# A two-layer encoder on one core: the products of U of layer 0 dealt out between those of the last four gate groups, the latents sent through DRAM, the w_ada tiles placed anew

## The chip, the core and the metric

The kernel runs on one core of a Trainium2 chip. The core has a matrix engine (TensorE, PE in the profile, with its weight loads as PEld), VectorE (DVE), ScalarE (ACT), GpSimd (POOL) and SyncE (SP), which here issues most DMAs. The metric is the device time of one execution in microseconds (us), the median over several runs. All results of TensorE go to PSUM, eight banks of 128 partitions by 512 words, from which VectorE and ScalarE take them.

## The reference

```python
for l in range(DEPTH):                       # DEPTH = 2, 512 positions, D = 2048
    mod = c_act @ w_ada[l] + b_ada[l]        # w_ada[l]: 2048 x 6144
    shift, scale, gate = jnp.split(mod, 3, axis=-1)
    h = _layernorm(x) * (1.0 + scale[:, None, :]) + shift[:, None, :]
    p = h @ w_in[l]
    u_f, z_f, cq, ckv, k_r, z_a = jnp.split(p, split_pts, axis=-1)  # 1024, 1024, 512, 256, 64, 1024
    y_f = _fourier_mix(u_f, w_fmix[l]) * jax.nn.silu(z_f)
    q = (_rmsnorm(cq, q_norm[l]) @ w_q_b[l]).reshape(B, S, N_HEADS, QK_HEAD_DIM)
    ...
    k_rope = _apply_rope(k_r, cos, sin)
    y_a = _mla_attention(q_nope, q_rope, k_nope, k_rope, v) * jax.nn.silu(z_a)
    y = jnp.concatenate([y_f, y_a], axis=-1) @ w_out[l]
    x = _layernorm(DEEPNORM_ALPHA * x + gate[:, None, :] * y, ln_g[l], ln_b[l])
```

All values are float32. `_fourier_mix` is a Fourier transform over the 512 positions and over the 128 channels of each of eight groups, real part, then a linear map for each group.

## The kernel before

Every float32 product is made of three products (`mm3`, L151 to L153) of a high and a low half; `split` makes the halves, the high one as a cast on ScalarE (L147) and the low one as a subtraction on VectorE (L148). So each weight tile is loaded by SP into `wr`, cast, subtracted, and then used.

**Layer 0, w_in.** The modulation of layer 0 comes out of w_ada, which is read while w_in is already worked on. So w_in is taken in five steps of 1, 2, 3, 4 and 6 blocks of 128 rows (`SZ`). Each step goes through six groups of columns: CQ (512 columns), CKV (320), and four gate groups of 512, ZF (two, for the Fourier half) and ZA (two, for attention). The sums of a group are added up in SBUF from step to step (L1063), except CQ, whose four banks are kept. In the last step the order is CQ, CKV, ZA0, ZA1, ZF0, ZF1 (`LAST`), each of three units of two row blocks; a gate unit is 24 products 512 wide, so a group 72.

**w_ada.** A tile of w_ada (512 KB) is scaled by c and added to a sum by VectorE (L247). `k_group` asks for tiles by credits (`bg_step`): in steps 0 to 3 those that the next step needs at an even pace, then `ZP` for each unit; in the last step `ZL` for each unit; `AP` in attention, `CP` in the output projection. When a block of tiles is complete, `finish` runs two or three calls of `bg_step` later: transposes on TensorE (L260), a reduction (L261) and an addition (`modT`, L221) on VectorE. The next step starts with `make_h`, which is ScalarE's scaling by `modT` (L364) and a split.

**U.** U is h times the 1024 columns of u_f, with the channels of each group folded into sums and differences (`fold_unit`, 16 units of one row block, each two operations of VectorE at L401 and L402, a split 1024 wide, and `xacc`, L412); h is folded over positions too (`first_eo`, L613 to L615, and a split 512 wide). In before, all 16 units stand in one place (`u_pass`) behind the last gate group and the small products of `folded_constants` (L539): for each of two halves of positions three products go into one bank of the pool `pa` with 264 columns, three into another with 504, and three into a bank of `pm` with 256, so 18 products a unit. `pa` and `pm` have four banks each. Then come the evacuation of U, `fourier_folded` (its first products are those of `pa` 256 wide and `pm` 258 wide), the rotary queries, and attention.

**Latents.** `latent_q` and `latent_kv` evacuate and normalise the results of CQ and CKV; their second parts transpose them (`to_feat`) as work between the units of the next group (`runner`). `rotary_key` (L853 to L858) stands in between.

**Order.** All units of weights stand in one `Stream`; taking one also loads and converts those that stand some places ahead (`st.ahead(raw, conv)`: two converted ahead at first, `UA0` before and in U). The conversions of the units to come are so written ahead of the products of the unit taken, and of what evacuates their banks. The build makes one fixed order for each engine out of that; each engine works through its own and waits for the others by semaphores.

## Time and profile before

| what | value |
|---|---|
| time before, three runs | median 1418.49 us (1417.31 to 1423.09) |
| profiled execution | 1409.84 us, span 1408.0 us |
| PE busy in the span | 1317.0 us (94%) |
| DVE, ACT, POOL busy | 1040.7 us (74%), 601.2 us (43%), 59.6 us (4%) |
| chain that ended last | PE 38%, issue 4%, DVE 2%, DMA 2%, ACT 1% |

The span runs from the first to the last instruction of the profiled execution; 1.84 us of its time lie outside. A product's busy time is longer than its distance to the next one, since they overlap, so short waits of PE don't show in its busy share; where products follow each other, the distance of their starts is the measure. In lists by time a number in brackets is what the engine stood idle before that row, and what ended it.

### The profile page before, as it was taken

What the parts mean: (1) busy time and instruction counts of PE and PEld (TensorE: products, weight loads), DVE (VectorE), ACT (ScalarE), POOL (GpSimd) and SP (SyncE); (2) the same over time, 40 slices, a digit from 0 to 9 for tenths busy, and PEclk for the clock granted to TensorE, in tenths of its full rate; (3) what the DMA queues carried; (4) which work ended last, traced back from release to release, by engine and by line L of the source; (5) the groups of instructions that cost most, each with busy time, mean ns of one, the idle gap of its engine ahead of it and who ended that gap; (6) DMA issues with size and microseconds to landing.
All of it is one profiled execution on the core that took longest, in us unless ns stands there. A gap on an engine that the chain in (4) does not pass through costs nothing. (4 is left out here: it accounts for less than half of the span.)

```text
span 1408.0 us, 18682 instructions
## 1 busy us (share of the span) xinstructions
PE 1317.0 (94%) x6837; PEld 1114.3 (79%) x6837; DVE 1040.7 (74%) x1748; ACT 601.2 (43%) x1131; POOL 59.6 (4%) x87
## 2 busy tenths in 40 slices
PE   4889999998698999999997999999999999999996
PEld 3767788877587888787876888887898888888885
DVE  7999994779987898689878758557755577632448
ACT  6621333655526776211147525323234677721210
POOL 1000000010000000000021001011100000000001
PEclk9999999999999999999998999999999999999998
DMA  8989872565665245988736435359544221263313
GB/s 272 327 272 309 298 248 85 165 200 180 193 224 164 69 162 194 326 307 318 275 115 224 157 102 164 106 199 354 175 124 118 78 67 53 75 240 103 92 60 120
DMA packets 134772, 257.45 MB, mean 183 GB/s; under 512 B 19532, under 2 KB 50392, under 8 KB 134680
## 3 DMA queue, kind: packets, MB, share of 16 engines
q1 hardware_dynamic: 127640, 232.92, 50.3%
q0 software_dynamic: 7040, 23.34, 4.8%
q8 instruction: 54, 0.88, 0.2%
q14 instruction: 38, 0.31, 0.1%
HBM read 239.42 MB, written 16.79 MB: 182 GB/s over the span
## 5 line engine op out<-in xcount | busy, mean ns | idle before, releaser
L151 PE MATMUL pa<-b,b 128*128 128x512 f32 (+3 forms) x1472 | 549.4, 376 | 30.2 <-ACT b L147 16.3
L152 PE MATMUL pa<-b,b 128*128 128x512 f32 (+3 forms) x1472 | 549.3, 373 | 7.2 <-DVE ln_v L188 4.3
L153 PE MATMUL pa<-b,b 128*128 128x512 f32 (+3 forms) x1472 | 546.7, 372 | 0.5 <-DVE b L148 0.5
L151 PEld LDWEIGHTS pa<-b,b 128*128 128x128 f32 x1472 | 278.6, 191 | 83.5 <-ACT b L147 23.7
L152 PEld LDWEIGHTS pa<-b,b 128*128 128x128 f32 x1472 | 279.9, 190 | 54.1 <-DVE b L148 5.9
L153 PEld LDWEIGHTS pa<-b,b 128*128 128x128 f32 x1472 | 279.4, 190 | 47.6 <-DVE b L148 1.9
L147 ACT CAST b<-wr 128x1024 fp32r<-128x1024 f32 (+3 forms) x166 | 162.6, 991 | 325.8 <-PE pa L153 173.8
L148 DVE TENSOR_TENSOR b<-wr,b 128x1024 fp32r<-128x1024 f32 (+3 forms) x166 | 188.7, 1144 | 132.9 <-PE pa L152 68.6
L247 DVE SCALAR_TENSOR_TENSOR acc<-ada,cact,acc 128x1024 f32<-128x1024 f32 (+2 forms) x193 | 226.6, 1181 | 14.6 <-DMA ada<-in_w_ada_dram 12.6
L151 PE MATMUL pm<-b,b 128*128 128x256 f32 (+3 forms) x500 | 167.5, 335 | 7.2 <-DVE b L1063 5.7
L152 PE MATMUL pm<-b,b 128*128 128x256 f32 (+3 forms) x500 | 161.9, 324 | 0.0
L153 PE MATMUL pm<-b,b 128*128 128x256 f32 (+3 forms) x500 | 161.6, 323 | 0.0
L151 PEld LDWEIGHTS pm<-b,b 128*128 128x128 f32 x500 | 96.4, 193 | 19.5 <-issue 4.8
L153 PEld LDWEIGHTS pm<-b,b 128*128 128x128 f32 x500 | 96.4, 193 | 6.8
L152 PEld LDWEIGHTS pm<-b,b 128*128 128x128 f32 x500 | 96.5, 193 | 6.5
L148 DVE TENSOR_TENSOR b<-pm,b 128x512 fp32r<-128x512 f32 (+4 forms) x104 | 60.7, 606 | 22.7 <-ACT b L147 22.3
L147 ACT CAST b<-pm 128x512 fp32r<-128x512 f32 (+4 forms) x104 | 51.8, 529 | 50.5 <-PE pm L751 28.6
L147 ACT CAST b<-b 128x1024 fp32r<-128x1024 f32 (+1 forms) x48 | 43.2, 912 | 60.2 <-DVE b L402 50.0
L148 DVE TENSOR_TENSOR b<-b,b 128x1024 fp32r<-128x1024 f32 (+1 forms) x48 | 49.5, 1042 | 13.8 <-ACT b L147 13.8
L147 ACT CAST b<-t 128x512 fp32r<-128x512 f32 (+1 forms) x81 | 40.9, 531 | 26.3 <-DVE t L1021 13.7
L148 DVE TENSOR_TENSOR b<-t,b 128x512 fp32r<-128x512 f32 (+1 forms) x81 | 45.0, 576 | 8.2 <-ACT b L147 7.9
L987 ACT ACTIVATE t<-pa,mx 128x512 f32<-128x512 f32 x64 | 44.1, 695 | 4.8 <-DVE mx L984 4.7
(180 smaller groups left out, 1251.7 us busy)
## 6 DMA issues: line engine op xcount, KB each, us to landing
wr<-in_w_in_dram SPq DMA_DIRECT2D x107, 512.0 KB, 3.9
ada<-in_w_ada_dram SPq DMA_DIRECT2D x96, 512.0 KB, 5.8
wr<-in_w_out_dram SPq DMA_DIRECT2D x64, 512.0 KB, 4.4
ada<-in_w_ada_dram SPq DMA_DIRECT2D x96, 256.0 KB, 4.7
ada<-in_w_ada_dram POOLq DMA_DIRECT2D x32, 512.0 KB, 5.4
b<-in_x_dram SPq DMA_DIRECT2D x16, 512.0 KB, 6.7
t<-szd SPq DMA_DIRECT2D x32, 256.0 KB, 4.2
ada<-in_w_ada_dram SPq DMA_DIRECT2D x32, 192.0 KB, 4.4
```

The lines of the kernel that those rows point to most:

```text
L147: A.copy(hi, src)
L148: V.tensor_tensor(lo, src, f(hi), op=ALU.subtract)
L151: PE.matmul(o, lh, rh, start=first, stop=False)
L152: PE.matmul(o, lh, rl, start=False, stop=False)
L153: PE.matmul(o, ll, rh, start=False, stop=last)
L247: V.scalar_tensor_tensor(out=a, in0=t[:, r - r0], scalar=cact[:, r:r + 1], in1=a, op0=ALU.mult, op1=ALU.add)
L987: A.activation(e, ps, AF.Exp, bias=mx, accum_out=ssum)
```

## The change

The 16 units of U go between the twelve units of the last four gate groups: after gate unit m, `UPAT[m]` units of U (0, 1, 1, 2, 1, 1, 2, 2, 1, 2, 1, 2). Their sums stay open all that time, in all four banks of `pm`; each bank holds 260 columns of the even half and 252 of the odd half, so a unit is 24 products 260 or 252 wide. The transposes of the latents would need `pm`, so `latent_q` and `latent_kv` write the normalised latents to DRAM and read them back ahead of the last gate group, where the rotary key and the loads for `folded_constants` stand now too. Behind U come its evacuation, `folded_constants` and the transposes. In layer 1, U takes the same four banks and 24 products a unit. The numbers for w_ada change: `ZP` from 0.3 to 0, `ZL` from 0.5 to 1.6 but only in CQ and CKV of the last step, with none in its four gate groups, `AP` from 1.2 to 1.4, `CP` from 2.3 to 2.4. Two memsets go from VectorE to GpSimd.

```diff
-    ZP, ZL, AP, CP, G0, G1 = 0.3, 0.5, 1.2, 2.3, 0.8, 1.6
+    ZP, ZL, AP, CP, G0, G1 = 0.0, 1.6, 1.4, 2.4, 0.8, 1.6
...
-    FW, UAH, UA0, YS = 2, 6, 4, 4
+    FW, UAH, UA0, YS = 2, 6, 3, 4
+
+    UPAT = [0, 1, 1, 2, 1, 1, 2, 2, 1, 2, 1, 2]
...
         def conv(t):
             if act is not None:
-                h[k] = act(k)
+                he[k] = act(k)
             w, hi, lo = big([P, 1024], F32), big([P, 1024]), big([P, 1024])
             c = t.rearrange("p (g c) -> p g c", c=P)
             e = w[:, 0:512].rearrange("p (g c) -> p g c", c=64)
...
     for l in range(DEPTH):
         if l == 0:
             for k0, nk in STEPS:
-                for g in FIRST if k0 + nk < NK else LAST:
+                last, m, ku = k0 + nk == NK, 0, 0
+                for g in LAST if last else FIRST:
                     for k, n in pairs(k0, nk):
                         st.add(dense(w_in[l], k * P, *g, n))
-            for k in range(NK):
-                st.add(fold_unit(w_in[l], k, lambda k: first_eo(k)))
+                        if last and g in ZA + ZF:
+                            for _ in range(UPAT[m]):
+                                st.add(fold_unit(w_in[l], ku, lambda k: first_eo(k)))
+                                ku += 1
+                            m += 1
             for k in range(2):
                 st.add(wq_unit(l, 4 * k, 4, 128, 64))
         else:
...
         yf = []
-        def u_pass():
-
-            e, o, b = [pa(), pa()], [pa(), pa()], [pm(), pm()]
-            for k in range(NK):
-                wh, wl = st.next()
-                for p in range(2):
-                    es, os_ = slice(p * P, p * P + P), slice(256 + p * P, 256 + p * P + P)
-                    for bank, ts, cs in ((e[p], es, slice(256, 520)), (b[p], es, slice(0, 256)),
-                                         (o[p], os_, slice(520, 1024))):
-                        mm3(bank[:, :cs.stop - cs.start], h[k][:, 0, ts], h[k][:, 1, ts], wh[:, cs], wl[:, cs],
-                            k == 0, k == NK - 1)
+        def u_start():
+            return [[pm(), pm()] for _ in range(2)]
+
+        def u_step(banks, k):
+
+
+            wh, wl = st.next()
+            hk = (h if l else he)[k]
+            for p in range(2):
+                for x in range(2):
+                    ts = slice(256 * x + p * P, 256 * x + p * P + P)
+                    n = 252 if x else 260
+                    for b in range(2):
+                        cs = slice(520 * x + b * n, 520 * x + b * n + n)
+                        mm3(banks[p][b][:, 260 * x:260 * x + n], hk[:, 0, ts], hk[:, 1, ts], wh[:, cs], wl[:, cs],
+                            k == 0 and x == 0, k == NK - 1 and x == 1)
+
+        def u_finish(banks):
             un = big([P, 2, 2, 2, P])
             GP.memset(f(un), 0.0)
             ue, uo = [], []
             for p in range(2):
+                a, b = banks[p]
                 t = big([P, 2, 512])
-                split(t[:, 0, 256:512], t[:, 1, 256:512], e[p][:, 0:256])
-                split(un[:, 0, p, 0, 120:128], un[:, 0, p, 1, 120:128], e[p][:, 256:264])
+                split(t[:, 0, 0:260], t[:, 1, 0:260], a[:, 0:260])
+                split(t[:, 0, 260:512], t[:, 1, 260:512], b[:, 0:252])
+                split(un[:, 0, p, 0, 120:128], un[:, 0, p, 1, 120:128], b[:, 252:260])
                 ue.append(t)
-            for p in range(2):
                 t = big([P, 2, 8, 64])
-                split(t[:, 0, :, 1:64], t[:, 1, :, 1:64], o[p][:, :504].rearrange("p (g c) -> p g c", c=63))
-                for a in range(2):
-                    V.memset(f(t[:, a, :, 0]), 0.0)
+                for i, ps in enumerate((a, b)):
+                    gs = slice(4 * i, 4 * i + 4)
+                    split(t[:, 0, gs, 1:64], t[:, 1, gs, 1:64], ps[:, 260:512].rearrange("p (g c) -> p g c", c=63))
+                for x in range(2):
+                    GP.memset(f(t[:, x, :, 0]), 0.0)
                 uo.append(t.rearrange("p a g c -> p a (g c)"))
-            for p in range(2):
-                split(ue[p][:, 0, 0:256], ue[p][:, 1, 0:256], b[p][:, 0:256])
             onesr = t2([P, P], F32R)
             V.memset(f(onesr), 1.0)
...
         cq, ckv, krs = [], [], []
+        def stash(p, i, n):
+            for tb in range(NT):
+                SP.dma_start(lat[i * NT + tb, :, :n], p[tb][:, :n])
+
+        def unstash(i, n):
+            t = [big([P, 2, n], F32) for _ in range(2)]
+            p = [t[tb // 2][:, tb % 2] for tb in range(NT)]
+            for tb in range(NT):
+                SP.dma_start(p[tb], lat[i * NT + tb, :, :n])
+            return p
+
         def latent_q(src):
             p = latent(src, 512, 512)
+            if l == 0:
+                stash(p, 0, 512)
+                yield
+                p = unstash(0, 512)
             yield
             cq.extend(to_feat(p, k) for k in range(4))
         def latent_kv(src):
             p = latent(src, 256, 320)
+            if l == 0:
+                stash(p, 1, 320)
+                yield
+                p = unstash(1, 320)
             kb = rotary_key(p)
             yield
             ckv.extend(to_feat(p, k) for k in range(2))
...
                         w = st.next()
                         p_ = min(pace, left[0])
                         left[0] -= p_
-                        bg_step(p_ if p_ > 0 else 0 if g == LAST[-1] and final else ZL if final else ZP)
+                        bg_step(p_ if p_ > 0 else ZP if not final else ZL if g in (CQ, CKV) else 0)
                         if g in ZF or g in ZA:
                             fm_half(banks, w, h, k, k == k00, k + nr == k01)
                         else:
...
                 lq = latent_q(k_group(CQ, keep))
                 next(lq)
-                lkv = latent_kv(k_group(CKV, pas(), runner(lq)))
+                lkv = latent_kv(k_group(CKV, pas()))
                 next(lkv)
+                finish_late()
+                st.ahead(4, UA0)
+                ub, ku, todo_u = None, 0, iter(UPAT)
+
+                def u_steps():
+                    nonlocal ub, ku
+                    for _ in range(next(todo_u)):
+                        if ub is None:
+                            ub = u_start()
+                        u_step(ub, ku)
+                        ku += 1
+
                 for i, (g, dst) in enumerate(zip(LAST[2:], (0, 1, 2, 3))):
                     if i == 3:
-                        finish_late()
-                        st.ahead(4, UA0)
-                    zs = k_group(g, pas(), runner(lkv) if i == 0 else lambda: None)
+                        next(lq)
+                        next(lkv)
+                        raw = constants_raw(0)
+                    zs = k_group(g, pas(), u_steps)
                     for j in range(4):
                         A.activation(zs[j], zs[j], AF.Silu)
                     spill(dst, zs)
+                st.ahead(4, 2)
+                u = u_finish(ub)
+                cw, nq, dt = folded_constants(0, raw)
+                drain(lq)
                 drain(lkv)
-                cw, nq, dt = folded_constants(0)
-                u = u_pass()
-                st.ahead(4, 2)
                 fb, rq = fourier_folded(u), rotary_queries(1)
                 for i in range(8):
                     next(fb, None)
...
             unfolded(banks, H)
             cw, nq, dt = folded_constants(1)
             st.ahead(4, 2)
-            fb = fourier_folded(u_pass())
+            ub = u_start()
+            for k in range(NK):
+                u_step(ub, k)
+            fb = fourier_folded(u_finish(ub))
             unfolded(fm_group(runner(fb, FW)), H + 4)
             drain(fb)
             gt = gates()
```

Lines of the changed kernel stand some lines lower: L148 is L150 there, L247 is L250, L260 and L261 are L263 and L264, L364 is L367, L412 is L415, L539 is L550, L1063 is L1101.

The first place is TensorE where the third of the five steps ends (ZA1, `pm`) and the fourth begins. These rows of before are the end of ZA0 of the third step, with the transposes of the modulation behind it and ZA1 still to come (`acc` is the sum of w_ada tiles):

```order
L151 MATMUL pm_1205<-b_923,b_1172 128x512
L152 MATMUL pm_1205<-b_923,b_1172 128x512
L153 MATMUL pm_1205<-b_923,b_1173 128x512
L260 MATMUL pm_1274<-ident,acc_866 128x128 x4
L260 MATMUL pm_1280<-ident,acc_866 128x128 x4
L151 MATMUL pm_1263<-b_913,b_1206 128x512
L152 MATMUL pm_1263<-b_913,b_1206 128x512
```

And these are the end of ZA1 of the third step in the changed kernel, with CQ of the fourth step (`pa`, the halves of h in b_1331) behind it:

```order
L153 MATMUL pm_1261<-b_919,b_1237 128x512
L263 MATMUL pm_1300<-ident,acc_928 128x128 x4
L154 MATMUL pm_1261<-b_919,b_1237 128x512
L155 MATMUL pm_1261<-b_919,b_1238 128x512
L153 MATMUL pm_1262<-b_919,b_1237 128x512
L154 MATMUL pm_1262<-b_919,b_1237 128x512
L155 MATMUL pm_1262<-b_919,b_1238 128x512
L263 MATMUL pm_1306<-ident,acc_928 128x128 x4
L153 MATMUL pa_366<-b_1263,b_1331 128x512
L154 MATMUL pa_366<-b_1264,b_1331 128x512
```

The transposes went from ahead of ZA1 to its end, directly ahead of the products that need h of the fourth step.

On VectorE, the rows that follow those transposes in the changed kernel are the reductions (L264), the last two additions to ZA1's sums, `modT`, two tiles of w_ada, and the low halves of h:

```order
L264 TENSOR_REDUCE red_1299<-pm_1306 128x4
L1101 TENSOR_TENSOR b_595<-b_595,pm_1262 128x512
L224 TENSOR_TENSOR modT_133<-red_1299,vecT 128x2x4
L250 SCALAR_TENSOR_TENSOR acc_1355<-ada_1460,cact,acc_1355 128x1024
L250 SCALAR_TENSOR_TENSOR acc_1355<-ada_1464,cact,acc_1355 128x1024
L150 TENSOR_TENSOR b_1331<-t_1329,b_1331 128x512
L150 TENSOR_TENSOR b_1336<-t_1334,b_1336 128x512
```

In before the same rows have one tile of w_ada ahead of `modT` and two behind it, and ZA1's own additions stand behind the halves of h.

The third place is VectorE where the second of the four gate groups of the last step is taken out of its banks. In before (ZA1's banks pa_2363 to pa_2366) the weights of the units ahead are already split:

```order
L148 TENSOR_TENSOR b_2510<-wr_2434,b_2509 128x1024
L148 TENSOR_TENSOR b_2540<-wr_2480,b_2539 128x1024
L1063 TENSOR_TENSOR b_593<-b_593,pa_2363 128x512
L1063 TENSOR_TENSOR b_593<-b_593,pa_2364 128x512
L1063 TENSOR_TENSOR b_594<-b_594,pa_2365 128x512
L1063 TENSOR_TENSOR b_594<-b_594,pa_2366 128x512
L148 TENSOR_TENSOR b_2589<-wr_2513,b_2588 128x1024
```

In the changed kernel (ZA1's banks pa_2412 to pa_2415) they stand behind the whole conversion of a unit of U and inside that of the next, which are the ninth and tenth of the sixteen:

```order
L415 SCALAR_TENSOR_TENSOR xacc_2199<-b_2741,orow,xacc_2199 128x520
L150 TENSOR_TENSOR b_2743<-b_2741,b_2742 128x1024
L150 TENSOR_TENSOR b_2783<-t_2778,b_2783 128x512
L404 TENSOR_TENSOR b_2786<-wr_2751 128x8x63
L1101 TENSOR_TENSOR b_594<-b_594,pa_2412 128x512
L405 TENSOR_TENSOR b_2786<-wr_2751 128x504
L1101 TENSOR_TENSOR b_594<-b_594,pa_2413 128x512
L415 SCALAR_TENSOR_TENSOR xacc_2199<-b_2786,orow,xacc_2199 128x520
L1101 TENSOR_TENSOR b_595<-b_595,pa_2414 128x512
L150 TENSOR_TENSOR b_2788<-b_2786,b_2787 128x1024
L1101 TENSOR_TENSOR b_595<-b_595,pa_2415 128x512
```

So four operations of the evacuation moved from a place with nothing but dense splits around them into the row of operations that convert U.

## Rows read from the trace of the kernel before

**Rows 1.** Busy time by stretch, with granted clock (PEclk) and DMA share.
```profile
core 0: us, PE busy (x) PEld busy (x) DVE busy (x) ACT busy (x) POOL busy (x), PEclk, DMA share, GB/s
215.00:242.00 27.00, 26.69 (x143) 23.05 (x142) 10.30 (x16) 9.77 (x20) 1.02 (x1) 1.00 0.24 71
...
262.70:279.00 16.30, 16.30 (x73) 13.52 (x72) 10.08 (x13) 8.44 (x13) 0.00 (x0) 1.00 0.76 238
...
340.00:376.00 36.00, 26.76 (x144) 19.82 (x144) 34.45 (x51) 16.71 (x39) 0.95 (x1) 1.00 0.60 175
...
400.00:440.00 40.00, 32.27 (x206) 28.66 (x205) 34.59 (x88) 14.32 (x38) 0.00 (x0) 0.91 0.66 224
...
880.00:900.00 20.00, 20.00 (x125) 17.82 (x124) 14.61 (x27) 8.56 (x18) 0.95 (x1) 1.00 0.45 134
```

**Rows 2.** PE by time, from the start of U to the first product behind it.
```profile
start us, us, engine line op out<-in xcount [idle before <-releaser]
316.44 0.68 PE L151 MATMUL pa<-b,b 128*128 128x264 f32 x1
...
374.05 0.28 PE L152 MATMUL pm<-b,b 128*128 128x256 f32 x1
...
374.28 0.39 PE L152 MATMUL pa<-b,b 128*128 128x504 f32 x1
...
374.74 0.28 PE L152 MATMUL pa<-b,b 128*128 128x264 f32 x1
...
374.98 0.28 PE L152 MATMUL pm<-b,b 128*128 128x256 f32 x1
...
375.44 0.39 PE L153 MATMUL pa<-b,b 128*128 128x504 f32 x1
381.13 0.55 PE L151 MATMUL pa<-b,b 128*128 128x256 f32 x1 [5.30 <-DVE b L148]
```

**Rows 3.** DVE by time, one unit of U (322.05 to 326.57).
```profile
322.05 0.42 DVE L614 TENSOR_TENSOR t<-t 128x256 f32<-128x256 f32 x1
...
323.52 0.35 DVE L425 SCALAR_TENSOR_TENSOR b<-pm,ident,b 128x128 fp32r<-128x128 f32 x1
323.78 0.68 DVE L148 TENSOR_TENSOR b<-t,b 128x512 fp32r<-128x512 f32 x1
...
326.57 1.28 DVE L247 SCALAR_TENSOR_TENSOR acc<-ada,cact,acc 128x1024 f32<-128x1024 f32 x1
```

**Rows 4.** Groups by form, PE from 311 to 317.
```profile
L539 PE MATMUL pm<-b,b 128*128 128x512 f32 x12 | 5.3, 595 | 0.0
```

**Rows 5.** Groups by form, DVE: splits from 244.7 to 311.7, then from 316 to 376.
```profile
line engine op names shapes xcount | busy us, mean ns | idle before us <-releasers
L148 DVE TENSOR_TENSOR b<-wr,b 128x1024 fp32r<-128x1024 f32 x10 | 12.2, 1221 | 7.8 <-ACT b L147 7.8
...
L148 DVE TENSOR_TENSOR b<-t,b 128x512 fp32r<-128x512 f32 x4 | 2.8, 689 | 2.7 <-ACT b L147 2.6
...
L148 DVE TENSOR_TENSOR b<-b,b 128x1024 fp32r<-128x1024 f32 x12 | 14.6, 1219 | 1.6 <-ACT b L147 1.6
```

**Rows 6.** DVE by time at the end of the third step.
```profile
136.05 2.73 DVE L1063 TENSOR_TENSOR b<-b,pm 128x512 f32<-128x512 f32 x4 [0.24 <-PE pm L153]
138.70 1.28 DVE L261 TENSOR_REDUCE red<-pm 128x4 f32<-128x512 f32 x2
...
143.73 1.29 DVE L148 TENSOR_TENSOR b<-t,b 128x512 fp32r<-128x512 f32 x2
```

**Rows 7.** PE, DVE and ACT by time where the second step ends.
```profile
87.61 0.82 PE L260 MATMUL pm<-ident,acc 128*128 128x128 f32 x6
93.25 0.80 PE L151 MATMUL pa<-b,b 128*128 128x512 f32 x1 [4.82 <-ACT b L147]
...
88.85 1.01 DVE L261 TENSOR_REDUCE red<-pm 128x4 f32<-128x512 f32 x2
...
90.97 0.16 DVE L221 TENSOR_TENSOR modT<-red,vecT 128x6 f32<-128x6 f32 x1
...
91.17 1.52 ACT L364 ACTIVATE t<-b,modT 128x512 f32<-128x512 f32 x2 [18.86 <-DVE modT L221]
```

**Rows 8.** Busy time by stretch, columns as in rows 1.
```profile
93.20:100.00 6.80, 6.75 (x17) 5.00 (x18) 6.80 (x9) 3.79 (x6) 0.00 (x0) 0.58 0.90 296
...
160.00:170.00 10.00, 7.31 (x41) 6.59 (x40) 9.85 (x14) 1.13 (x2) 0.00 (x0) 0.86 1.08 359
```

More of the change, by code (lines that the diff above doesn't have):

```diff
@@ L199, in trunk_kernel @@
     szd = drp.tile([2 * H, P, S], F32, name="szd")
+    lat = drp.tile([2 * NT, P, 512], F32, name="lat")
     gated = drp.tile([DEPTH, D], F32, name="gated")
@@ L513, in fm_half, with constants_raw, folded_constants @@
                     first and i == 0, last and i == nr - 1)
-    def folded_constants(l):
+    def constants_raw(l):
+        cc = big([P, 2, P], F32)
+        GP.dma_start(cc, chan.rearrange("a p c -> p a c"))
+        wf = big([P, G, P], F32)
+        SP.dma_start(wf, w_fmix[l].rearrange("g m d -> m g d"))
+        return cc, wf
+    def folded_constants(l, raw=None):
         def keep(shape, dt=F32R):
@@ L525, in folded_constants @@
         cw, nq, dt = [[None, None], [None, None]], [], []
-        cc = big([P, 2, P], F32)
-        GP.dma_start(cc, chan.rearrange("a p c -> p a c"))
-        wf = big([P, G, P], F32)
-        SP.dma_start(wf, w_fmix[l].rearrange("g m d -> m g d"))
+        cc, wf = raw or constants_raw(l)
         for hf in range(2):
@@ L603, in trunk_kernel @@
     finish_late()
-    h = [None] * NK
+    h, he = [None] * NK, [None] * NK
     for k in range(SZ[0]):
```

## The prediction

> **What bounds the kernel now.** PE is busy in nearly the whole span, so the first view is the busy time by stretch, read for stretches in which PE is not. The one that the change touches is U: from 340 to 376 DVE works 34.45 of 36 us and PE shows 26.76, at a full granted clock [rows 1]. Busy time understates the loss, since products overlap, so I take the distances of starts. The last whole pass through the three kinds of product lasts from 374.05 to 374.98, 0.93 for two of each, so a unit of 18 takes 6 x 0.465 = 2.79 us and 16 units 44.6 us. But the first product of U starts at 316.44 and the last one ends its turn 0.23 behind 375.44: 59.2 us [rows 2]. So 14.6 us are lost there, in DVE's pace: a unit costs DVE 326.57 - 322.05, less the foreign row from 323.52 to 323.78, 4.26 us, and a tile of w_ada between units 1.28 more [rows 3]. Behind U, PE stands idle 5.30 us, until DVE has split the evacuated banks [rows 2]. That makes 19.9 us that U costs over its products. Ahead of it there is room: from 215 to 242 (CQ and CKV of the last step) DVE is busy 10.30 of 27 us, and in the 16.3 us of ZA1 10.08 [rows 1].
>
> **The change part by part.**
>
> *U between the groups.* A group holds PE 16.3 us [rows 1] and asks little of DVE; a unit of U holds it 2.79 us and asks 4.26. Mixed, four groups and 16 units are 65.2 + 44.6 = 109.8 us of PE. DVE's part: 16 x 4.26 = 68.2, twelve splits of gate weights at 1.22 [rows 5], 14.6, and sixteen evacuations at 0.66 (2.65 for four, [rows 6]), 10.6: together 93 us, and a few for the rotary key. So DVE no longer sets the pace, and no w_ada tile stands in it. **-19.9 us**, before what follows.
>
> *24 products for 18.* The columns stay 1024 for a half of positions. Two products 256 wide take 0.23 (374.05 to 374.28), two 504 wide 0.46, two 264 wide 0.24 [rows 2]: 0.115 to 0.12 each for the new widths, so 24 take 2.76 to 2.88 us against 2.79. I take the upper half, 0.05 a unit: **+0.8 us** in layer 0, and as much in layer 1, where PE is never idle around U (20.00 of 20, [rows 1]) and every added product counts: **+0.8**.
>
> *Evacuations behind conversions.* Banks of `pa` are four, and a group takes all, so the next group's first unit waits for the four additions into the sums, which now stand in DVE's row behind conversions of U (the third place of the order above). Count it for ZF0, the worst. From the last addition of ZA0 to the last of ZA1 DVE has six units of U, four gate splits and four additions: 6 x 4.26 + 4 x 1.22 + 2.65 = 33.1 us. PE has between the same two points (ZA1's units, six units of U less those that stand ahead, and ZF0's first unit) some 29 to 30. Counted through in this way from CKV on, PE waits about 1.9 us at the first unit of ZA1 and 3.8 us at that of ZF0; at ZF1 only three units of U have come between, and DVE is ahead again. **+5.7 us**, with 3 and 10 as bounds: the lower if the additions overtake a conversion's wait for ScalarE, the upper if each conversion waits half a microsecond for its cast, which is what splits 512 wide waited in before (2.7 us for 4, [rows 5]).
>
> *What now stands behind U.* `folded_constants` (12 products of 5.3 us busy, [rows 4], 4.7 by starts) and 32 transposes move from ahead of U to behind it: no more work than before. But they need banks of `pm`, all four of which hold U, so they start when the first bank is evacuated, some 2 us, and later wait a little for each other's banks; against that, they cover the 5.30 us that I have counted as removed. **+2.5 us**, bounds 1.5 and 5.
>
> *Stash and read back.* 1.6 MB out and in on SP's queue. The writes wait for the normalised latents, and a load of weights stands behind them; three are in flight by then, and DMA is at a share of 0.24 there [rows 1]. The reads wait for a buffer, and only the rotary key on DVE waits for them, at a point where DVE is ahead of PE. **0**, up to 2 if the key's row on DVE holds the conversions behind it. The memsets on GpSimd: 0, hidden by the evacuation.
>
> At the first product of the Fourier stage the sum is 19.9 - 0.8 - 5.7 - 2.5, **about 11 us gained**.
>
> *The tiles of w_ada behind it.* By DVE's order 76 tiles stand ahead of the rotary queries, for 82 before, and 92 ahead of the first scores, for 96. So the stage between them has 16 tiles where it had 14: 2.5 us more DVE work in a stretch in which DVE is busy 34.59 of 40 us and PE loses most of 8 [rows 1]. **+1.5**, bounds 0 and 2.5. The four tiles that go into the scores I cost at 0, since PE is saturated there and DVE isn't; without that cover 5.
>
> *ZP from 0.3 to 0.* This is the term that the change's words don't show. With fewer credits the last w_ada block for the fourth step is complete later, and its transposes come at the end of ZA1 of the third step, directly ahead of CQ of the fourth, which needs h. In before they stand a whole group ahead: the reductions run at 138.70 and the split of h at 143.73, while ZA1 keeps PE busy [rows 6]. What it looks like without that cover is the end of the second step: six transposes at 87.61, reductions at 88.85, `modT` at 90.97, ScalarE at 91.17, and PE stands 4.82 us until 93.25 [rows 7]; then it runs for 6.80 us at a granted clock of 0.58 [rows 8], most of that time at the lower level (1.2 of 2.4 GHz), 2.9 us lost. In the changed order no tile stands ahead of `modT`, which saves 1.2, but two stand ahead of the low halves of h, and an addition lies between the reductions: 4.8 us again, and the clock's 2.9. Against it: from 160 to 170, in the fourth step, PE is busy 7.31 of 10 us at a clock of 0.86, 4.1 us lost to DVE [rows 8]; DVE has two or three tiles less ahead of that point, and gains the 4.8 us, so I take this as repaid. **+3.6 us**, bounds 0.7 (no drop of the clock) and 7.7 (nothing repaid).
>
> *UA0, AP, CP*: order only; work in attention and the output projection that PE hides. 0.
>
> **Sum:** -11 + 0.8 + 1.5 + 3.6 = **-5 us**: 1404.8 for the profiled execution of 1409.84. The median shown stands 8.65 above that execution, so the forecast is 1413.5.
>
> **The rivals.** *First, the third step's end costs nothing net*: `modT` comes without a tile ahead of it, the clock holds, and the fourth step repays the wait. For it: DVE's work is only moved. Against it: the wait in [rows 7]. Then -8.5 to -10: 1409. *Second, DVE's gain is given back*: the 19.9 us are DVE's deficit, and if the evacuations take 10, the banks behind U 5, the Fourier stage 2.5 and the third step 7.7 us, 19.9 - 26.8 leaves nothing; half of these overruns give 1418. *Third, slower: DVE stays the bound of the merged stretch.* In before DVE stood idle ahead of ten gate splits for 7.8 us and ahead of four of U for 2.7, waiting for ScalarE's casts; in the dense row of U it was 1.6 for 12 [rows 5]. If each of the 12 + 16 conversions kept the idle time of the first kind, 0.7 to 0.8 us, that is 21 us more in a DVE sum of 93 plus the key: 115 to 120 against PE's 110. It decides from about 0.5 us a conversion. U would end some 13 us later than forecast: +8, 1426.
>
> *A fourth, by the clock.* The many short waits of PE from 340 to 376, a quarter of its time, left the clock at 1.00, while the single waits of 4.82 and 5.30 us were followed by lower clocks [rows 1, 2, 7, 8]. If the waits at ZA1 and ZF0, some 7 and 9 us from the first wait to the last, ran at half clock, they would cost at most 8 us more: 1421. By the rows this is unlikely, 3 in 100. The Trainium skill, page "TensorE: Matmul & The Clock Gate", section "A second HAM failure mode: psum-queue depth-cycling", says that idling in small bits between groups that cycle through PSUM banks is enough to make the clock go up and down; by that rule this rival would be the likely one and the time 1421, where the rows give 1413.5. The trace does not agree so far: U's own short waits came at 1.00.
>
> **How the numbers follow.** What can be told from no change here is 0.5%, 7 us. Forecast (-1.5 to -7.5) 0.42, most of it within 7 us; first rival 0.31, mostly beyond; second 0.12; third 0.12; fourth 0.03. Faster 0.38, same 0.47, slower 0.15. The range reaches from the first rival with a cheaper ZF0 (1404) to between the second and third, 1425; the forecast's own is 1410 to 1417.
>
> **What would show it.** U's last product at about 359, with PE waits for L1101 of about 2 us near 265 and 4 us near 295; a first Fourier product at 370 to 374; a PE wait of 4 to 5 us near 147, released by ScalarE's cast, and a lower clock behind it; no wait near 165; DVE under 18 of 20 us between 320 and 360. The prediction fails if U ends behind 366, if the wait at 147 is under 2 us, or if the stretch behind U is longer than 15 us.

## The result: 0.9 to 1.4% slower, where 0.3% faster was forecast

The changed kernel took 1431.86 us (median of 4, 1430.39 to 1432.99) against 1417.9 for the kernel before (median of 4): a ratio of 1.0091, 95% interval 1.0064 to 1.0119. Twice more, beside kernels of before in longer series, it gave 1.0144 (1.0112 to 1.0177) and 1.0140 (1.0109 to 1.0171). So it is slower by some 14 to 21 us, and 1431.86 lies outside the range of the forecast, which ended at 1425.

The profiled execution took 1431.62 us, its span 1429.8, which is 21.8 above the span shown of before. A second profile of before (the first of the runs below) has a span of 1416.5, so some 8 us of that difference lie in which execution was profiled. The stretches show where the rest is. Points are starts on PE: of the sixth of the eight transposes ahead of the last step (L260), and the first of the cosines' row of ones (L751), of the scores, of layer 1's `folded_constants` and cosines, and of the last product.

| stretch, us | before, two profiles | changed, three profiles | difference of means | forecast |
|---|---|---|---|---|
| start to transposes | 192.8, 194.0 | 197.6, 200.5, 199.4 | +5.8 | +3.6 |
| to cosines | 193.9, 193.9 | 195.9, 195.9, 195.7 | +1.9 | -11 |
| to scores | 54.1, 54.0 | 56.2, 56.3, 57.2 | +2.5 | +1.5 |
| to constants of layer 1 | 406.5, 409.6 | 408.0, 407.8, 406.8 | -0.5 | 0 |
| to cosines of layer 1 | 56.9, 57.0 | 68.9, 69.1, 67.7 | +11.6 | +0.8 |
| to the last product | 491.7, 495.9 | 491.1, 491.5, 491.4 | -2.5 | 0 |

Two rows are far off: the stretch of the gate groups and U, by 13 us, and layer 1's U, by 11.

### The profile after

The busy time by stretch of the changed kernel (columns as in [rows 1]):

```profile
240.00:260.00 20.00, 20.00 (x117) 18.11 (x116) 15.76 (x33) 10.20 (x26) 1.60 (x2) 1.00 0.58 185
260.00:280.00 20.00, 17.74 (x104) 15.25 (x103) 20.00 (x33) 14.38 (x29) 0.00 (x0) 1.00 0.65 197
280.00:300.00 20.00, 19.33 (x120) 17.18 (x118) 19.41 (x31) 12.26 (x28) 0.00 (x0) 1.00 0.59 178
300.00:320.00 20.00, 16.89 (x87) 14.79 (x88) 17.24 (x23) 10.41 (x21) 0.00 (x0) 0.83 0.64 192
320.00:340.00 20.00, 16.67 (x108) 15.13 (x107) 13.09 (x45) 7.01 (x16) 0.79 (x1) 0.97 0.62 191
340.00:360.00 20.00, 20.00 (x104) 17.22 (x104) 15.49 (x26) 11.52 (x23) 1.18 (x5) 0.86 0.60 171
360.00:380.00 20.00, 16.97 (x98) 14.06 (x97) 8.60 (x23) 6.95 (x19) 3.99 (x6) 0.91 0.70 226
380.00:400.00 20.00, 16.73 (x99) 11.91 (x98) 17.34 (x43) 10.97 (x28) 0.00 (x0) 1.00 0.25 80
```

The dense row of U, with DVE at 34.45 of 36 us, is gone. In its place DVE is full from 260 to 300, at the front of the groups, and slack behind 320. PE's clock, 1.00 through U before, is 0.83 and 0.86 in two of these stretches, part of them at the lower of its two levels. PE's waits from 240 to 400 (in all, times, longest, in us) show why:

```profile
PE pa L153 <- DVE b L1101: 9.3, 3, 3.8
PE pm L755 <- ACT b L149: 2.9, 1, 2.9
PE pm L862 <- DVE b L150: 1.8, 2, 1.6
PE pm L550 <- DVE b L548: 0.5, 1, 0.5
```

The last two are waits of the transposes and of the constants behind U. And these are the products behind the four waits, by time:

```profile
271.04 0.47 PE L153 MATMUL pa<-b,b 128*128 128x512 f32 x1 [2.24 <-DVE b L1101]
...
303.12 0.77 PE L153 MATMUL pa<-b,b 128*128 128x512 f32 x1 [3.78 <-DVE b L1101]
...
339.59 0.76 PE L153 MATMUL pa<-b,b 128*128 128x512 f32 x1 [3.33 <-DVE b L1101]
...
376.19 0.63 PE L755 MATMUL pm<-b,t 128*128 128x256 f32 x2 [2.92 <-ACT b L149]
```

These are the first products of ZA1, ZF0 and ZF1, and the first behind U. The product behind the second wait lasts 0.77 us and that behind the third 0.76, where 0.47 stands behind the first: the clock has fallen. The wait at ZF1 begins on DVE, whose row there is:

```profile
323.10 1.23 DVE L150 TENSOR_TENSOR b<-b,b 128x1024 fp32r<-128x1024 f32 x1 [0.80 <-ACT b L149]
330.40 0.19 DVE L872 TENSOR_TENSOR t<-b,cos_t 128x32 f32<-128x32 f32 x1 [6.08 <-DMA b<-lat]
...
338.76 0.69 DVE L1101 TENSOR_TENSOR b<-b,pa 128x512 f32<-128x512 f32 x1
```

DVE stands 6.08 us for the latents that are read back, then makes the rotary key, and the additions of ZF0 come at 338.76, behind that. In layer 1 PE's row is:

```profile
857.74 3.59 PE L550 MATMUL pm<-b,b 128*128 128x512 f32 x8
861.84 1.96 PE L550 MATMUL pm<-b,b 128*128 128x512 f32 x4 [0.50 <-DVE fc L558]
...
866.26 0.36 PE L153 MATMUL pm<-b,b 128*128 128x260 f32 x1 [2.47 <-DVE fc L558]
...
872.02 0.56 PE L153 MATMUL pm<-b,b 128*128 128x260 f32 x1 [1.54 <-DVE fc L428]
```

and the busy time there:

```profile
860.00:880.00 20.00, 15.49 (x75) 12.80 (x74) 17.75 (x34) 10.61 (x29) 3.26 (x5) 0.74 0.61 173
```

`folded_constants` has the four banks of `pm` in turn, and U now needs all four: its first product waits 2.47 us for a bank and a later one 1.54, until DVE has taken the constants out, and the clock from 860 to 880 is 0.74. Before, U needed two of `pm`, and PE waited for nothing there.

### The profile page after: what moved, and what is told of

It reads as the page before. It is cut to its first block, busy times and chain, and to the rows that moved or that the text cites. A ratio compares the mean times of both kernels' runs of the same rounds, so it can differ in the third digit from the quotient of the medians.

```text
span 1429.8 us, 19111 instructions
## 1 busy us (share of the span) xinstructions
PE 1326.3 (93%) x7029; PEld 1129.9 (79%) x7029; DVE 1041.0 (73%) x1744; ACT 602.3 (42%) x1135; POOL 59.7 (4%) x95
## 5 line engine op out<-in xcount | busy, mean ns | idle before, releaser
L153 PE MATMUL pa<-b,b 128*128 128x512 f32 (+2 forms) x1344 | 509.8, 381 | 33.2 <-ACT b L149 13.7
L154 PE MATMUL pa<-b,b 128*128 128x512 f32 (+2 forms) x1344 | 508.6, 379 | 5.1 <-DVE ln_v L190 5.1
L155 PE MATMUL pa<-b,b 128*128 128x512 f32 (+2 forms) x1344 | 506.5, 378 | 0.5 <-DVE b L150 0.5
L153 PEld LDWEIGHTS pa<-b,b 128*128 128x128 f32 x1344 | 256.1, 191 | 82.7 <-ACT b L149 19.9
L154 PEld LDWEIGHTS pa<-b,b 128*128 128x128 f32 x1344 | 257.9, 192 | 46.5 <-DVE ln_v L190 5.3
L155 PEld LDWEIGHTS pa<-b,b 128*128 128x128 f32 x1344 | 257.3, 192 | 46.8 <-DVE b L150 2.4
L150 DVE TENSOR_TENSOR b<-wr,b 128x1024 fp32r<-128x1024 f32 (+3 forms) x166 | 188.8, 1145 | 133.2 <-PE pa L154 61.0
L250 DVE SCALAR_TENSOR_TENSOR acc<-ada,cact,acc 128x1024 f32<-128x1024 f32 (+2 forms) x193 | 226.9, 1183 | 22.5 <-DMA ada<-in_w_ada_dram 20.6
L153 PE MATMUL pm<-b,b 128*128 128x256 f32 (+5 forms) x692 | 221.5, 320 | 8.3 <-DVE b L1101 3.7
L154 PE MATMUL pm<-b,b 128*128 128x256 f32 (+5 forms) x692 | 215.8, 312 | 0.0
L155 PE MATMUL pm<-b,b 128*128 128x256 f32 (+5 forms) x692 | 215.7, 312 | 0.0
L153 PEld LDWEIGHTS pm<-b,b 128*128 128x128 f32 x692 | 132.8, 192 | 21.0 <-issue 8.6
L154 PEld LDWEIGHTS pm<-b,b 128*128 128x128 f32 x692 | 133.1, 192 | 6.9
L155 PEld LDWEIGHTS pm<-b,b 128*128 128x128 f32 x692 | 132.9, 192 | 6.6
L150 DVE TENSOR_TENSOR b<-pm,b 128x512 fp32r<-128x512 f32 (+6 forms) x120 | 66.1, 574 | 38.8 <-ACT b L149 38.3
L149 ACT CAST b<-pm 128x512 fp32r<-128x512 f32 (+5 forms) x120 | 56.6, 499 | 65.4 <-PE pm L770 29.4
L150 DVE TENSOR_TENSOR b<-b,b 128x1024 fp32r<-128x1024 f32 (+1 forms) x48 | 49.6, 1044 | 15.3 <-ACT b L149 15.3
L150 DVE TENSOR_TENSOR b<-t,b 128x512 fp32r<-128x512 f32 (+1 forms) x81 | 45.2, 578 | 9.3 <-ACT b L149 9.3
L1027 ACT ACTIVATE t<-t,ssum 128x512 f32<-128x512 f32 x64 | 45.3, 735 | 1.7 <-DVE ssum L1026 1.7
```

The lines of the kernel that those rows point to most:

```text
L149: A.copy(hi, src)
L150: V.tensor_tensor(lo, src, f(hi), op=ALU.subtract)
L153: PE.matmul(o, lh, rh, start=first, stop=False)
L154: PE.matmul(o, lh, rl, start=False, stop=False)
L155: PE.matmul(o, ll, rh, start=False, stop=last)
L250: V.scalar_tensor_tensor(out=a, in0=t[:, r - r0], scalar=cact[:, r:r + 1], in1=a, op0=ALU.mult, op1=ALU.add)
```

## The experiments

**The kernel before, once more.** No edit.

> The kernel before, unaltered, for a second profile. If the 4 us by which the changed kernels are behind already at 90 us come from the change (ZP, w_ada), the second step's transposes run at 88 again; if they differ from run to run (a lower clock near 46 in every profile of the changed kernel, whose order up to there is nearly the same), this one may show them at 89 to 92 too, with the lower clock.

1418.26 us, span 1416.5. The second step's transposes start at 91.6 (87.6 in the first profile), so the 4 us by which the changed kernel is behind there need not be the change's. Ahead of the last step the two profiles of before are only 1.2 us apart. The execution on which the forecast was worked out was 8 us shorter than this one.

**Layer 1's banks.**

```diff
-            return [[pm(), pm()] for _ in range(2)]
+            return [[pa() if l else pm(), pm()] for _ in range(2)]
```

> The changed kernel with one line altered: in layer 1 the four banks of U come two from pa and two from pm, as many of each as leave folded_constants two banks of pm; the 24 products a unit stay. Theory A (layer 1 loses 11 us because U's four banks of pm wait for those of folded_constants, 2.5 and 1.5 us, and the clock then halves): about 10 us less than the changed kernel, 1422 us, and no lower clock between 858 and 880. Rival B (24 narrow products cost more than 18): no more than 1 us less. Rival C (the w_ada numbers AP and CP): no change.

1423.53 us, ratio to before 1.0078 (1.0047 to 1.0109). From layer 1's constants to its cosines 61.7 us instead of 67.7 to 69.1, so the profile gives back 6 to 7 with one line, though the 24 products are still there. Of the waits for a bank one is left (1.5 us), and the one behind U (2.2). Rival B falls.

**The other way round: the kernel before with the new U in layer 1 alone.** `u_start`, `u_step` and `u_finish` of the change, called in layer 1; layer 0 keeps `u_pass`.

```diff
-            fb = fourier_folded(u_pass())
+            ub = u_start()
+            for k in range(NK):
+                u_step(ub, k)
+            fb = fourier_folded(u_finish(ub))
```

> The kernel before with only layer 1's U changed: 24 products a unit into four shared banks of pm, directly behind folded_constants. Theory A: 8 to 11 us slower than before (a wait of 4 us for the banks, a lower clock behind it, 2 us behind U), 1.006 to 1.008. Rival B (only the number of products): 1 us, within the measurement. If the wait is there but is repaid: within 3 us.

1423.57 us, ratio 1.0081 (1.0050 to 1.0113): 10 to 11 us. The waits of PE from 845 to 925, where before has none:

```profile
PE pm L151 <- DVE fc L547: 2.5, 1, 2.5
PE pm L739 <- ACT b L147: 2.2, 1, 2.2
PE pm L151 <- DVE fc L425: 1.1, 1, 1.1
```

So layer 1's part costs some 10 us by itself. It isn't repaid.

**The key ahead of the stash.**

```diff
             p = latent(src, 256, 320)
+            kb = rotary_key(p)
             if l == 0:
-                stash(p, 1, 320)
+                stash(p, 1, 256)
                 yield
-                p = unstash(1, 320)
-            kb = rotary_key(p)
+                p = unstash(1, 256)
```

> The changed kernel with the rotary key made ahead of the stash, as the latents come, so that nothing on DVE waits for the latents to be read back. Theory A2 (DVE's idle 6 us for the read-back makes the additions of ZF0 late, so PE waits 3.3 us at ZF1 and the clock halves behind it): 5 to 7 us less, about 1425 us, no PE wait at ZF1. Rival (additions are late because of the conversions ahead of them, as at ZA1 and ZF0): the wait at ZF1 stays above 2 us and the time within 2 us.

1430.24 us, ratio 1.0117 (1.0096 to 1.0138), no clear gain, where 1425 was expected. The wait at ZF1 is gone, as expected, but that at ZF0 is 7.5 us now; PE waits for the additions 9.9 us in all:

```profile
PE pa L153 <- DVE b L1101: 9.9, 2, 7.5
```

**The additions written ahead of the next units of U.** In `k_group`:

```diff
-                        work()
+                        if k + nr < k0 + nk:
+                            work()
+                    if g == CQ or not final:
+                        work()
...
                             V.tensor_tensor(s_[tb], s_[tb], banks[tb][:, :n], op=ALU.add)
+                    if g != CQ and final:
+                        work()
                     return s_
```

> The changed kernel with the additions of a gate group written ahead of the units of U that follow it, so that DVE takes the banks out before it converts the next units of U. Theory A3 (the waits at ZA1, ZF0 and ZF1, 2.2, 3.8 and 3.3 us, come from the place of the additions behind conversions, and the halved clock behind two of them costs 3.4 us each): up to 9 us of waits and 7 of clock less, 1417 to 1422 us. Rival (DVE is the bound of the stretch, 93 us and its waits against 110): the waits move to the next gate units and the time stays within 3 us.

1432.89 us, ratio 1.0138 (1.0108 to 1.0167), no gain. ZA0's additions came a unit of U sooner on DVE, but ZA1's stood at nearly the same place again (from 302.93, where the changed kernel has 302.29); ZA1's wait went, ZF0's grew to 7.5, and in all it is 11.3. Together with the run before: the waits can be moved about, their sum stays near 10. That points to a debt of DVE up to 305, not to the place of one operation; the next run tries it.

**Fewer units of U at the front.**

```diff
-    UPAT = [0, 1, 1, 2, 1, 1, 2, 2, 1, 2, 1, 2]
+    UPAT = [0, 0, 0, 1, 1, 1, 1, 2, 2, 2, 3, 3]
```

> The changed kernel with UPAT [0,0,0,1,1,1,1,2,2,2,3,3], so that fewer units of U stand between the first gate units. Theory D (PE's 10 us of waits at the gate groups are DVE's debt: it is busy 20 of 20 us from 260 to 300 because nine units of U are dealt out by the first unit of ZF0, whatever the order of the additions): waits at ZA1 and ZF0 under 2 us together, U ends 6 to 10 us sooner, 1418 to 1422 us. Rival (place of the additions behind the conversions): waits stay at 8 to 10 us in all, and the time too.

The changed kernel beside it:

> The changed kernel itself, unaltered, as the mark for the others on the same chip: between 1.006 and 1.012 of before, 1422 to 1431 us.

1425.57 us against 1434.11 for the changed kernel beside it (1.0096, 1.0062 to 1.0130, against 1.0144). The waits for additions fall from 9.4 to 1.7 us, so theory D holds for the waits, and U's last product starts at 359.78 instead of 375.94. The time fell by 8.5 us and missed the 1418 to 1422 that were expected, since the wait behind U grows from 2.9 to 8.2:

```profile
PE pm L755 <- ACT b L149: 8.2, 1, 8.2
...
PE pa L153 <- DVE b L1101: 1.7, 1, 1.7
```

Of the 16 us that U ends sooner 2.6 stand already at the transposes ahead of the last step; of the other 13.6 the cosines get 6.9 (189.0 us behind those transposes for 195.9). DVE's lateness comes out at the end of U instead.

**The w_ada numbers.** ZP alone, in two series (in the second beside the changed kernel), and the new numbers and their rule in the kernel before.

```diff
-    ZP, ZL, AP, CP, G0, G1 = 0.0, 1.6, 1.4, 2.4, 0.8, 1.6
+    ZP, ZL, AP, CP, G0, G1 = 0.3, 1.6, 1.4, 2.4, 0.8, 1.6
```

and in the kernel before:

```diff
-    ZP, ZL, AP, CP, G0, G1 = 0.3, 0.5, 1.2, 2.3, 0.8, 1.6
+    ZP, ZL, AP, CP, G0, G1 = 0.0, 1.6, 1.4, 2.4, 0.8, 1.6
...
-                        bg_step(p_ if p_ > 0 else 0 if g == LAST[-1] and final else ZL if final else ZP)
+                        bg_step(p_ if p_ > 0 else ZP if not final else ZL if g in (CQ, CKV) else 0)
```

> The changed kernel with ZP back at 0.3, so that the transposes for the fourth step stand a group earlier. If the wait of 4 us behind the third step and the lower clock behind it are a net cost, 3 to 4 us less, about 1428 us, and the fourth step begins without a wait. If they are repaid by 180 us, as the profiles suggest (4.3 us behind before at both 88 and 180), no change within 2 us.

> The changed kernel itself once more, as the mark for the two others in five rounds: 1.009 to 1.015 of before.

> The changed kernel with ZP at 0.3, in five rounds beside the mark. If only the end of the third step is repaid or not: 0 to 2 us less than the mark. If tiles that are done early also spare waits in the output projection (PE waited 3.2 us there for sums behind tiles in the changed kernel): 4 to 6 us less.

> The kernel before with only the w_ada numbers and their rule as in the change (ZP 0, ZL 1.6 in CQ and CKV alone, AP 1.4, CP 2.4), U as it was. If the numbers cost: 2 to 4 us slower than before, a wait near 147. If they help by themselves (no tiles in U's dense row, which is 5 x 1.2 us less for DVE there): U's 59 us fall by some 5, 2 to 6 us faster.

With ZP 0.3: 1423.83 us, 1.0070 (1.0051 to 1.0089), then 1425.61, 1.0098 (1.0073 to 1.0122), where the changed kernel beside it has 1432.69: 7 us, more than was expected. The kernel before with the numbers: 1416.31, 1.0023 (1.0004 to 1.0041), as expected 3 us slower. The end of the third step in the changed kernel looks as forecast. PE by time:

```profile
148.33 0.66 PE L263 MATMUL pm<-ident,acc 128*128 128x128 f32 x4
152.86 0.79 PE L153 MATMUL pa<-b,b 128*128 128x512 f32 x1 [3.87 <-ACT b L149]
```

DVE by time:

```profile
150.58 0.17 DVE L224 TENSOR_TENSOR modT<-red,vecT 128x8 f32<-128x8 f32 x1
150.65 2.60 DVE L250 SCALAR_TENSOR_TENSOR acc<-ada,cact,acc 128x1024 f32<-128x1024 f32 x2
```

The busy time by stretch:

```profile
140.00:160.00 20.00, 16.13 (x64) 12.21 (x62) 19.58 (x24) 7.20 (x11) 0.00 (x0) 0.83 0.78 264
160.00:170.00 10.00, 10.00 (x54) 8.91 (x53) 7.94 (x10) 3.40 (x4) 0.00 (x0) 1.00 0.98 315
```

A wait of 3.87 us, a lower clock behind it, and nothing lost from 160 to 170, where [rows 8] show 7.31 of 10 and 0.86. With ZP 0.3 the wait is gone. Where the 7 us lie is shown in part only. Up to the last step's transposes the two profiles with ZP 0.3 are 3.6 us ahead of the three of the changed kernel on average, but 1.8 of them stand already at the second step's transposes. From the scores to layer 1's constants those with ZP 0.3 take 402.9 and 404.2 us, the others 406.7 to 408.0: 4 us less. There, from 545 to 850, PE waits for sums that stand behind tiles on DVE (L1215): 3.2, 1.5 and 2.2 us in the profiles of the changed kernel, 0.7 and 0.6 with ZP 0.3. So these waits explain about 1.7 of the 4.

**All repairs.** Layer 1's `u_pass` of before, ZP 0.3, the key ahead of the stash, `folded_constants(0)` between CKV and the groups, the later UPAT. Of this, new are:

```diff
                 next(lkv)
                 finish_late()
+                cw, nq, dt = folded_constants(0)
...
-            ub = u_start()
-            for k in range(NK):
-                u_step(ub, k)
-            fb = fourier_folded(u_finish(ub))
+            fb = fourier_folded(u_pass())
```

> The changed kernel with layer 1's U as before, ZP 0.3, the rotary key ahead of the stash, folded_constants between CKV and the gate groups (its banks of pm are free there and DVE has room), and UPAT as in the later pattern. If the losses are those named (layer 1 10 us, waits and clock at the gate groups 10 to 15, the stretch behind U 6), it gains 20 to 28 us over the changed kernel: 1400 to 1407 us, 0.7% or so faster than before. If the stretch behind U keeps its 20 us and the waits only move, 1412 to 1416, the time of before.

1409.88 us, ratio 0.9979 (0.9962 to 0.9996): 24 us less than the changed kernel beside it, and barely under before: between the two times that were expected. Behind U PE stands 9.2 us; the view of its waits has the row

```profile
PE pm L758 <- ACT b L149: 9.2, 1, 9.2
```

and DVE by time, from the last split of U on:

```profile
365.34 1.23 DVE L150 TENSOR_TENSOR b<-b,b 128x1024 fp32r<-128x1024 f32 x1 [0.53 <-ACT b L149]
366.49 4.69 DVE L428 SCALAR_TENSOR_TENSOR b<-wr,vecT,b 128x256 fp32r<-128x256 f32 x10
371.09 2.47 DVE L1133 TENSOR_TENSOR b<-b,pa 128x512 f32<-128x512 f32 x4
374.52 0.43 DVE L150 TENSOR_TENSOR b<-pm,b 128x260 fp32r<-128x260 f32 x1 [0.96 <-ACT b L149]
```

U's last product starts at 369.32, and its evacuation (the row at 374.52) stands behind ten splits of w_q and ZF1's additions.

**w_q held back**, by `st.limit` at the units of w_q until `u_finish` is written; then, besides, **no trip through DRAM** (the latents are transposed between CKV and the groups), with the constants ahead of the groups and, in another run, behind U; and last **the constants between CQ and CKV**.

```diff
+                st.limit = wq0
...
                 u = u_finish(ub)
+                st.limit = None
+                st.start()
```

```diff
-                lkv = latent_kv(k_group(CKV, pas()))
+                lkv = latent_kv(k_group(CKV, pas(), runner(lq)))
                 next(lkv)
+                drain(lq)
+                drain(lkv)
```

> The version with all four repairs (layer 1's U as before, ZP 0.3, key and constants early, UPAT later), and besides the loads and conversions of w_q held back until U is evacuated. Theory E (the 9.2 us for which PE stands behind U come from DVE's ten splits of w_q, 4.7 us, and what follows them, which stand ahead of U's evacuation): the wait falls to about 5 us, the time by 3 to 5, 1405 to 1407 us where the version without this gave 1409.9. Rival (U's evacuation waits for its own last products, or w_q is then late for the rotary queries): no change within 2 us, a new wait near 390.

> As g1, but the latents aren't sent through DRAM: they are transposed between CKV and the gate groups, where pm is still free, and kept in SBUF. If the read back and the 32 transposes behind U cost what they take there (3.5 to 5 us behind a wait, against 3.5 us of PE ahead of the groups), 0 to 3 us less than g1; if the seven buffers kept longer make the conversions wait, slower than g1 by several us, with PE waits for b in the gate groups.

> As g3, but folded_constants behind U as in the changed kernel, where it can fill part of the wait for U's evacuation. The four repairs lost about 8 us on PE between 250 and 270, where the constants stood; if that is their price there, this is 2 to 5 us faster than g3; if their banks of pm wait for U's evacuation as in the changed kernel (5 us more behind U), equal or slower.

> The version with layer 1's U as before, ZP 0.3, the later UPAT, w_q held back and no stash, with folded_constants between CQ and CKV, where DVE is idle for 13 us. If constants behind U cost the 5 us for which they wait for U's banks, and constants behind CKV the 8 us for which DVE is late there, both go: 1400 to 1405 us, faster than the best so far (0.995 of before). If DVE's row behind CKV is as late as before, no change against it.

| version | us | ratio to before, interval | first cosine product behind U's last, us | transposes to scores, us |
|---|---|---|---|---|
| before (time of these series, first profile) | 1413 | 1 | 8.0 us | 248.0 |
| all repairs | 1409.88 | 0.9979 (0.9962 to 0.9996) | 18.2 | 246.7 |
| and w_q held | 1408.06 | 0.9961 (0.9932 to 0.9989) | 15.7 | 246.9 |
| and no stash | 1411.02 | 0.9968 (0.9946 to 0.9991) | 5.2 | 248.7 |
| no stash, constants behind U | 1407.02 | 0.9953 (0.9931 to 0.9975) | 19.1 | 245.9 |
| no stash, constants behind CQ | 1412.92 | 0.9998 (0.9976 to 1.0020) | 5.4 | 251.5 |

In the version with the constants behind U their products are part of the 19.1 us. Theory E holds for the wait (9.2 to 4.5 us); the 2 us that it gives are less than the 3 to 5 expected and not clear of the spread. The kernel runs without the stash and the read back: 3.0 us slower with the constants in the same place (1411.02 for 1408.06), and with the constants behind U 1.0 faster. The constants behind CQ did not bring the 1400 to 1405 us expected. And where the stretch behind U is shortest the scores come latest: the time comes back between cosines and scores. The version without the stash and with the constants behind U beats both kernels, before by 0.5% (0.25 to 0.69). The busy time over that whole stretch, first of before:

```profile
193.00:441.00 248.00, 225.31 (x1191) 188.51 (x1190) 199.66 (x396) 117.88 (x259) 10.10 (x12) 0.97 0.56 179
```

of the changed kernel:

```profile
197.60:449.70 252.10, 227.21 (x1288) 195.07 (x1287) 192.39 (x387) 116.75 (x259) 9.92 (x16) 0.95 0.55 173
```

and of this version:

```profile
195.00:441.00 246.00, 223.49 (x1290) 192.00 (x1289) 198.33 (x392) 118.61 (x261) 10.07 (x16) 0.97 0.55 174
```

From the last transposes to the first scores it takes 246 us where it took 248, with PE and DVE busy for nearly as long as before. So of U's 19.9 us dealing it out gains 2; the rest comes back elsewhere in that stretch. What is left of the gain lies between the scores and layer 1's constants, 402.7 us where the two profiles of before have 406.5 and 409.6: in the output projection this version waits for no sum behind tiles, and before 2.6 and 5.2 us between 560 and 740. That it comes from the tiles of ZP and AP together is argued from these waits, not tried apart.

## Why the prediction was wrong

**Which terms failed.** Four did: layer 1's U (+0.8 forecast, 11.6 measured), the waits at the gate groups (+5.7, 9.3 measured), the clock there (nothing, some 5) and the stretch behind U (+2.5, some 6). *"U between the groups ... -19.9 us"* was costed by DVE's sum over the stretch, 93 us of 110. The sum was about right (DVE is busy 100.2 us from 248 to 373, the rotary key and others among it). But it does not say when the work falls due: DVE converts three units ahead, so nine of the sixteen conversions of U stand ahead of the additions that ZF0 waits for (from 302.29), when PE has had six units. So DVE is full from 260 to 300 and has 7 of 20 us free from 320 to 340. In *"Evacuations behind conversions"* ZA1 and ZF0 came out as counted (2.24 and 3.78 for 1.9 and 3.8). ZF1, costed at nothing, waited 3.33. That is the term *"Stash and read back"*, 0, *"up to 2 if the key's row on DVE holds the conversions behind it"*: the forecast took the point to be one at which DVE is ahead, and DVE's 6 us of standing ate the lead. Yet without them the wait only went elsewhere, as the run with the key shows: in all 9.9 us for 9.3. The later UPAT brought it to 1.7.

**The clock.** The forecast charged the lower clock to the third step's end alone, and gave 3 in 100 to its showing at the groups. In all three profiles of the changed kernel it fell at the waits at ZF0, ZF1 and U's end. By the stretches, at most 3.4 us went so from 300 to 320 (0.17 of 20) and 2.8 from 340 to 360. The Trainium skill, page "TensorE: Matmul & The Clock Gate", section "A second HAM failure mode: psum-queue depth-cycling", tells of a clock that goes up and down because of small idle bits between groups that cycle through banks. What the rows show here is a fall at single waits of 2.9 to 3.8 us. Behind the wait of 2.24 at ZA1 there was none in this profile (the clock is 1.00 from 260 to 300), and in U of before, with many waits under 1 us, none either (1.00 from 340 to 376, [rows 1]). So the effect of the page's rule is there, its cause as told is not what these rows show.

**Behind U.** *"They cover the 5.30 us that I have counted as removed"* was the wrong half of that step: PE's row has the products of `xr` first, which wait 2.92 us for the evacuation, so nothing is covered, and the constants and transposes wait some 3 us more for banks. From U's last product to the cosines' row of ones it was 20.5 us (373.0 to 393.5), and 11.3 before. With the moved work (4.7 us of constants, 3.5 of transposes), less the 5.3 and with the 2.5 of the forecast it should have been 16.7. No run tried this stretch alone.

**Layer 1.** *"Every added product counts: +0.8"* asked what the products cost and not whose banks they take. The products cost what was forecast: 24 of them last 2.83 us (879.95 to 882.78 in the changed kernel), 2.79 before. Four banks for two cost 10, and this is the largest single term of the miss: the run of before with this change alone and the run with two of the banks from `pa` show it from both sides.

**The third step's end** was right in place, and nearly in size: a wait of 3.87 for 4.8, a lower clock, and the loss from 160 to 170 repaid. The kernel before with the numbers alone is 3 us slower, for +3.6. What the forecast left out is the output projection. In the changed kernel ZP 0.3 is worth 7, and where they come from is shown in part only.

**The rivals.** The third (DVE the bound of the merged stretch) is the nearest by time: it ended on the right side. Its mechanism (each conversion waits for ScalarE) is not what the runs showed. From 260 to 300 DVE hardly stood at all. By mechanism the second and the fourth come closer: the second's 10 us for the evacuations and 5 for the banks behind U are near what was measured, 9.3 and 6, and the clock of the fourth, given 3 in 100, did fall at ZF0. None of the four had layer 1.

**The signs.** U's last product came at 373.0, where 366 was named as failure, and the stretch behind U lasted 18.6 us (to 391.56), where 15 was. The waits at ZA1 and ZF0, the wait of ScalarE's cast at the third step's end and the slack of DVE from 320 to 360 came nearly as named, the first three some 6 to 8 us later.

Added up from the forecast's -5: layer 1 +11, waits at the groups +4, the clock there about +5, behind U +4, the start +2 (the three profiles of the changed kernel differ there by 2.9 us, so this can't be told from the spread): about 21, where the table has 19. Layer 1 is tried by itself; the others are read from profiles and rest on the repairs together, which take away 24.

## What to carry to other kernels

Before work is spread out to hide another engine's deficit, add that engine's work up step by step along the new order, not over the stretch; and look where the deficit comes out at the end, since here it reappeared behind U and before the scores. An accumulation that stays open holds its banks: ask of every one what else used them, ahead of it, behind it, and wherever else the same function is called. A wait of some microseconds on TensorE can cost more than itself, by the clock behind it.

## What had not been expected of the hardware

Single waits of PE of 2.9 to 3.9 us at the third step's end, at ZF0, at ZF1 and behind U came with the lower clock in every profile of the changed kernel, and before's U, with waits of 0.6 to 0.9 us in nearly every unit from 340 on, ran through at 1.00. The length of a wait alone does not decide it: in the second profile of before a wait of 3.54 us at 170 was followed by none (1.00 from 160 to 180). A wait of 2.2 us at ZA1 came with it in the run with layer 1's other banks (0.91 from 260 to 280) and with none in the three profiles of the changed kernel (1.00). A lower clock near 46 us shows in the second profile of before and in all profiles of the changed kernel but not in the first of before, which is 4 us ahead of the second at 88 us, 1.2 us at the transposes ahead of the last step and 8.5 at the end: two executions of one program differ by that much.
